# First 256 MLP features in plain products, in two token halves, and block sums on VectorE alone

## The chip, the cores and the metric

The kernel runs on one core of a Trainium2 chip. The metric is the device time of one execution in microseconds (us); before the change the median of three runs is 1396.17 us. TensorE (PE in the profile) multiplies, VectorE (DVE), ScalarE (ACT) and GpSimd (POOL) work on tiles, SyncE (SP) issues most transfers between HBM and the on-chip memory (SBUF). Each engine runs its own queue in order and waits on semaphores.

## What is computed

One layer of a hybrid encoder trunk on 1024 tokens with 1024 channels, in float32. The change lies between the output projection and the second MLP matrix:

```python
h = h + einsum('bse,ed->bsd', concat([y_a, y_b]), w_out)
z = einsum('bsd,df->bsf', rms_norm(h, norm2_g), w_ff1)      # 1024 -> 4096
h = h + einsum('bsf,fd->bsd', square(relu(z)), w_ff2)       # 4096 -> 1024
gate = sigmoid(einsum('bsd,de->bse', rms_norm(h, ple_norm_g), w_ple_gate))
h = h + gate * einsum('bsk,kd->bsd', p, w_ple_up)
```

## The kernel before, in words

Every float32 operand is split into a rounded high half (ScalarE, names ending in h) and the rest as a low half (VectorE, ending in l), and a product is three passes on TensorE: high x high, high x low, low x high. A matmul is 128x128 weights times 128x512 tokens.

The first MLP matrix (4096 features) is made in 16 blocks of 256 features, c = 0 to 15, from `products` and `sw_prods`. A block is a 2 x 2 split of features and channels against a 2 x 2 split of channels and tokens, done with seven products in place of eight (Strassen-Winograd): 7 products x 4 channel tiles x 3 passes = 84 matmuls. The token side (`sw_blocks`, four channel tiles j, each with its partner j + 4) has own blocks 11, 21, 22 and sums t1 to t4, all scaled by norm2_g, with a high and a low half; they stay in SBUF for all blocks. The weight side is made anew for each block (`sw_prep`): two raw transfers of 512 KB into tag wr (three buffers), own blocks a, sums s1 to s4 in four adds on SBUF (L231 to L234; on VectorE for c < 2, on GpSimd after that), and the split halves a, b, c, d in tags wh and wl (two buffers each).

The norm's factor is not needed before the end of a block: squares of h are summed in acc2 (L1198, L1199; ScalarE squares, GpSimd adds), `sumsq_to_rstd` sums over channels with small matmuls (tile n2ps) and takes the root, `bcast_rstd` spreads it with eight transposes (n2R) into Rb, and `finish(c)` multiplies relu(z) by it, squares, makes the sums that the second matrix wants (GpSimd, L1292 to L1298) and writes them to HBM (zd). The second matrix (`ff2_sweep`) reads them back (zr), its operands for three steps being fetched ahead by `ff2_early`.

In the last part of the output projection, products of channels 6 and 7 (op) run while the own blocks and sums of the first tiles are made. The order on each engine is set by a scheduler of the framework from program order and priorities; L1304 to L1346 are that program order.

Of the kernel before, what the change touches and what calls it, by code (L numbers as in the profile page):

```python
# [11 lines left out]
F32 = mybir.dt.float32  # L12
# [47 lines left out]
def tile_block(ctx, tc, xT, pT, w_in, w_out, w_ff1, w_ff2, w_gate, w_up, vecs, gate_b, rpbp, con,  # L60
# [179 lines left out]
        put(s1, 512, ("s1",), "d")  # L240
        return w

    def sw_prods(nm, w, B, z, part, ps_):


        pss = {}

        def prod(an, bn, js=range(4)):
            ps = pss.get(an)
            if ps is None:  # L250
                ps = pss[an] = ps_(f"{nm}_{an}_{bn}")
            elif js[-1] == 3:
                js = (3,)
            for j in js:
                for i, (x_, y_) in enumerate(passes(w[an][0][:, j], w[an][1][:, j], *B[bn, j])):
                    TE.matmul(ps, x_, y_, start=j == 0 and i == 0, stop=j == 3 and i == 2)  # L256
            return ps

        def add(o, a, b):
            mark["add"] = V.tensor_tensor(o, a, b, op=ALU.add).ins  # L260

        c11, c12, c21, u2 = z[0][:, 0:512], z[0][:, 512:], z[1][:, 0:512], z[1][:, 512:]
        if part == 2:
            for an, bn in (("11", "11"), ("12", "21"), ("s2", "t2"), ("s4", "22")):
                prod(an, bn, range(3))
        if part != 1:
            S.activation(u2, prod("11", "11"), AF.Copy)
            add(c11, u2, prod("12", "21"))
            add(u2, u2, prod("s2", "t2"))
        if part:  # L270
            add(c12, u2, prod("s4", "22"))
            add(u2, u2, prod("s3", "t3"))
            add(c21, u2, prod("22", "t4"))
            p5 = prod("s1", "t1")
            add(c12, c12, p5)
            add(u2, u2, p5)
# [912 lines left out]

    with tc.tile_pool(name="ff1", bufs=1) as ff1:  # L1190
        B = {}
        acc2 = utile32("acc2")

        sqs = []

        def sq_acc(acc, src):
            sqs.append(sqs[-2] if len(sqs) > 1 else utile32(f"sq2_{len(sqs)}"))
            S.activation(sqs[-1], src, AF.Square)  # L1198
            G.tensor_tensor(acc, acc, sqs[-1], op=ALU.add)  # L1199

        def b_alloc(nm, j):
            if len(B) < NB:
                t_ = ff1.tile([P, 2, 512], F32R, tag="b", bufs=NB, name=f"b{nm}_{j}")
            else:
                t_ = utile(f"b{nm}_{j}").rearrange("p (a b) -> p a b", a=2)
            return t_[:, 0], t_[:, 1]

        def blocks(j):
            h1, h2 = hres[j], hres[j + 4]
            tmp = utile32 if j > 1 else lambda n: wp.tile([P, T], F32, tag="wr", name=n, bufs=3)  # L1210
            sw_blocks(j, h1, h2, vcol(V_G2, j), vcol(V_G2, j + 4), tmp(f"ta{j}_"), tmp(f"tb{j}_"), b_alloc, B, True, G if j < 3 else V)
        def squares(ks):
            for k in ks:
                if k == 0:
                    S.activation(acc2, hres[k], AF.Square)
                else:
                    sq_acc(acc2, hres[k])
# [91 lines left out]
        blocks(0)  # L1309
        w4 = out_w((6, 7), range(4, 8))  # L1310
        run(out_proj((6, 7), range(4), ps_, w5))
        blocks(1)
        last = out_proj((6, 7), range(4, 8), ps_, w4)
        run(last, 25)
        squares((0, 4))
        blocks(2)
        run(last)
        w = prep(0)
        squares((1, 5))
        blocks(3)  # L1320
        squares((2, 6))
        with after("hi"):
            squares((3, 7))
        for e in range(8):
            dump(f"h1_{e}", hres[e])

        for c in range(NC_):
            if c:
                products(c, w, 0)
            else:  # L1330
                products(0, w, 2)
            if c == NC_ - 1:
                pre = [ff2_early(0)]
            if c == 1:
                bcast_rstd(rs2, range(KT), "n2")
                finish(0)
            if c:
                products(c, w, 1)
            else:
                rs2 = sumsq_to_rstd(acc2, range(KT), "n2")  # L1340
            if c + 1 < NC_:
                w = prep(c + 1)
            if c == NC_ - 1:
                pre += [ff2_early(1), ff2_early(2)]
            if c:
                finish(c)  # L1346


    with tc.tile_pool(name="ff2", bufs=2) as ff2:
# [226 lines left out]
```

## Time and profile before

| | us |
|---|---|
| median of 3 runs | 1396.17 (1395.35 to 1396.94) |
| the profiled execution | 1398.95 |
| its span in the trace | 1397.1 |
| mean granted clock of TensorE | 0.966 of full speed |
| TensorE busy | 1321.2 |
| VectorE busy | 914.1 |
| ScalarE busy | 591.5 |
| GpSimd busy | 545.7 |

TensorE's matmuls are pipelined: a row gives 0.39 us for one, but they start every 0.2267 us. A row of the timeline has a start, a duration, engine, line, operation, the tile written and the tiles read, and in brackets the idle time before it and the instruction whose end ended it.

### The profile page before, as it was taken

How to read it: one execution, taken by the hardware profiler on the slowest of the kernel's cores; microseconds unless marked ns; L12 is line 12 of the kernel's file. 1: busy time of each engine (PE TensorE's matmuls, PEld its weight loads, DVE VectorE, ACT ScalarE, POOL GpSimd, SP SyncE). 2: the span in 40 equal slices, each digit the busy share in tenths (PEclk: the TensorE clock that was granted, in tenths of full speed). 3: DMA queues.
4: the chain of work that ended last, by engine and by line, in shares of the span. 5: the costliest groups of instructions: out<-in, count | busy, mean ns of one | idle time of the engine just before them, and what ended most of it. 6: DMA issues, size and time to landing. Idle time of an engine off the chain costs nothing.

```text
span 1397.1 us, 19354 instructions
## 1 busy us (share of the span) xinstructions
PE 1321.2 (95%) x7115; PEld 1105.5 (79%) x7115; DVE 914.1 (65%) x1419; ACT 591.5 (42%) x971; POOL 545.7 (39%) x424
## 2 busy tenths in 40 slices
PE   7999999999998899996899999999999799999998
PEld 5988778799897667775678888888788678888887
DVE  4486886665672555669856666666648998559443
ACT  7353434264553545545333333333434334455321
POOL 2215676463331111116466555655202561007422
PEclk9999999999998799998899999999999999999999
DMA  8553333475322553311145444554876673542342
GB/s 288 198 152 83 117 112 106 149 250 165 112 62 99 168 165 129 117 48 45 32 165 160 141 150 136 159 166 158 303 273 224 196 254 94 171 147 72 106 143 83
DMA packets 153422, 206.03 MB, mean 147 GB/s; under 512 B 17776, under 2 KB 102768, under 8 KB 153328
## 3 DMA queue, kind: packets, MB, share of 16 engines
q1 hardware_dynamic: 144656, 185.77, 42.1%
q10 hardware_dynamic: 7200, 13.11, 2.8%
q0 software_dynamic: 1472, 5.92, 1.2%
q8 instruction: 56, 0.92, 0.3%
q14 instruction: 38, 0.31, 0.1%
HBM read 151.60 MB, written 53.17 MB: 147 GB/s over the span
## 4 chain that ended last, share of the span: by engine, by line
PE 56%; DMA 6%; DVE 6%; issue 3%; POOL 1%; ACT 1%; SPq 1%; DVEq 0%; POOLq 0%; ACTq 0%
PE f_P L1379 19%; PE p_s_t L256 9%; PE g L1448 6%; PE p L256 6%; PE op L1023 3%; PE p_s L256 3%; PE p_t L256 3%; DMA tab<-tabI 2%; PE pv L995 1%; DMA tab<-tabU 1%; PE o1p L310 1%; DMA nr<-qnd 1%; DMA wo_0r<-w_out 1%; DVE h L1025 1%; PE pt L975 1%
## 5 line engine op out<-in xcount | busy, mean ns | idle before, releaser
L1268 DVE TENSOR_TENSOR zl<-zr,zh 128x1024 fp32r<-128x1024 f32 x56 | 82.5, 1480 | 6.3 <-ACT zh L1267 6.3
L256 PE MATMUL p<-b,w_ah 128*128 128x512 f32 x256 | 80.3, 395 | 4.2 <-DVE b L193 4.2
L964 POOL TENSOR_SCALAR pc<-pc,st 128x288 f32<-128x288 f32 (+1 forms) x32 | 17.5, 548 | 160.9 <-DVE st L959 143.8
L1249 POOL TENSOR_TENSOR w2re<-sk,w2re 128x512 f32<-128x512 f32 x16 | 27.0, 1687 | 98.7 <-issue 62.9
L1267 ACT ACTIVATE zh<-zr 128x1024 fp32r<-128x1024 f32 x56 | 58.5, 1048 | 12.8 <-DMA zr<-zd 11.9
L260 DVE TENSOR_TENSOR z<-z,p_s_t 128x512 f32<-128x512 f32 x64 | 42.5, 686 | 32.2 <-PE p_s_t L256 30.9
L954 ACT ACTIVATE pc<-pc,st 128x288 f32<-128x288 f32 (+1 forms) x64 | 36.3, 569 | 57.6 <-DVE st L953 57.6
L256 PEld LDWEIGHTS p<-b,w_ah 128*128 128x128 f32 x256 | 48.7, 190 | 14.7 <-DVE b L193 4.6
L256 PE MATMUL p<-b,w_al 128*128 128x512 f32 x128 | 50.7, 398 | 9.3 <-DVE w_al L141 9.3
L1379 PE MATMUL f_P<-zl,w2h 128*128 128x512 f32 x128 | 52.3, 408 | 6.3 <-DVE zl L1268 6.3
L953 DVE CUSTOM_DVE_ANT_1 pc<-sc,tab 128x288 f32<-128x288 f32 (+1 forms) x64 | 29.9, 504 | 42.0 <-DMA tab<-tabU 17.6
L1402 POOL TENSOR_TENSOR h<-h,evP 128x512 f32<-128x512 f32 x8 | 14.8, 1886 | 98.3 <-ACT evP L1393 98.3
L788 POOL TENSOR_SCALAR wv<-vh,wj 128x129 f32<-128x129 f32 x56 | 30.6, 549 | 56.7 <-PE num L789 51.9
L1292 POOL TENSOR_TENSOR tz<-z,z 128x512 f32<-128x512 f32 x16 | 20.7, 1296 | 81.6 <-ACT z L1281 81.6
L1379 PE MATMUL f_P<-zh,w2h 128*128 128x512 f32 x128 | 51.1, 399 | 1.2 <-ACT zh L1267 1.2
L1448 PE MATMUL g<-gh,wg_h 128*128 128x512 f32 (+1 forms) x136 | 51.6, 380 | 0.0
L1379 PE MATMUL f_P<-zh,w2l 128*128 128x512 f32 x128 | 51.4, 401 | 0.0
L1448 PE MATMUL g<-gh,wg_l 128*128 128x512 f32 (+1 forms) x136 | 51.3, 377 | 0.0
L1448 PE MATMUL g<-gl,wg_h 128*128 128x512 f32 (+1 forms) x136 | 51.2, 377 | 0.0
L1280 DVE SCALAR_TENSOR_TENSOR z<-z,Rb 128x1024 f32<-128x1024 f32 x32 | 50.2, 1573 | 0.9 <-ACT Rb L180 0.9
L138 ACT ACTIVATE w_bh<-w_0r 128x1024 fp32r<-128x1024 f32 x16 | 17.0, 1063 | 73.0 <-POOL w_0r L234 53.3
L138 ACT ACTIVATE w_ah<-w_0r 128x1024 fp32r<-128x1024 f32 x16 | 17.0, 1061 | 68.4 <-PE p_t L256 68.4
(697 smaller groups left out, 4619.6 us busy)
## 6 DMA issues: line engine op xcount, KB each, us to landing
zr<-zd SPq DMA_DIRECT2D x56, 512.0 KB
zd<-z ACTq DMA_DIRECT2D x48, 256.0 KB
w2r<-w_ff SPq DMA_DIRECT2D x48, 256.0 KB
w_0r<-w_ff SPq DMA_DIRECT2D x16, 512.0 KB
w_1r<-w_ff SPq DMA_DIRECT2D x16, 512.0 KB
zd<-tz SPq DMA_DIRECT2D x32, 256.0 KB
zd<-z SPq DMA_DIRECT2D x32, 256.0 KB
w2re<-w_ff SPq DMA_DIRECT2D x16, 512.0 KB
```

What stands on the lines that cost most here:

```text
L138: mark["hi"] = S.activation(hi, raw, AF.Copy).ins
L256: TE.matmul(ps, x_, y_, start=j == 0 and i == 0, stop=j == 3 and i == 2)
L260: mark["add"] = V.tensor_tensor(o, a, b, op=ALU.add).ins
L788: G.tensor_scalar(wv, vh[:, c, 0:129], wj[:, col], 1.0, op0=ALU.mult, op1=ALU.mult)
L953: V.tensor_tensor_reduce(pb, sc.rearrange("p a b -> p (a b)"), tab[:, s], -1.0, -NEG, ALU.add, ALU.min, st[:, 0:1])
L954: S.activation(pb, pb, AF.Exp, scale=-1.0, bias=st[:, 0:1], accum_out=st[:, 1:2])
L1023: TE.matmul(ps, a, b, start=n == 0 and i == 0, stop=n == len(ks) - 1 and i == 2)
L1267: S.activation(hi, raw, AF.Copy)
L1268: dv.append(V.tensor_tensor(lo, raw, hi.bitcast(F32), op=ALU.subtract).ins)
L1280: V.scalar_tensor_tensor(z_, z_, 0.0, Rb, op0=ALU.max, op1=ALU.mult)
L1379: pe_last = TE.matmul(ps[n, e], a, b, start=st and k == 0, stop=sp and k == 2)
L1448: TE.matmul(ps, x_, y_, start=k == 0 and i == 0, stop=k == KT - 1 and i == 2)
```

## The change

Block 0 no longer uses sums. Its 256 features are computed as plain products, one token half (`plain("p0a")`, tokens 0 to 511, that is blocks 11 and 21 of the token side) right behind the output projection, before block 1, the other (`plain("p0b")`) behind block 15; 48 matmuls each. p0a's result is written to HBM and read back when the factor is known (in c = 3), and once more at the end to make block 0's sums. p0b (tokens 512 to 1023) needs block 22 and the blocks 12, made in c = 15 (four tiles), and its own copy of the weights, w1q.

`sw_blocks` is split into `own_blocks` (needed by p0a) and `sum_blocks`; all sums and low halves of the token side are on VectorE, and some are one 1024-wide instruction where two 512-wide ones stood. The squares come behind t1 of the last tile (`squares`), are added up in Rb itself, the first half of each on GpSimd and the second on VectorE, with one work tile. The norm's sum is taken in c = 2 behind its first three products, and it is spread, and block 1 finished, in the middle of the remaining products of c = 2.

```diff
-        def blocks(j):
-            h1, h2 = hres[j], hres[j + 4]
...
+        def own_blocks(j):
...
+            S.activation(hi, h2, AF.Copy, scale=g2)
+            V.scalar_tensor_tensor(lo, h2, g2, hi.bitcast(F32), op0=ALU.mult, op1=ALU.subtract)
+            B["21", j], B["22", j] = (h21, l21), (h22, l22)
+        def sum_blocks(j):
...
+            S.activation(t3, b12, AF.Copy, scale=g1)
+            V.scalar_tensor_tensor(t3, b22, g2, t3, op0=ALU.mult, op1=ALU.subtract)
+            V.scalar_tensor_tensor(t2, b11, g1, t3, op0=ALU.mult, op1=ALU.add)
+            V.scalar_tensor_tensor(t4, b21, g2, t2, op0=ALU.mult, op1=ALU.subtract)
+            (h2_, h4_, hi), (l2_, l4_, lo) = b_alloc(f"th_{j}"), b_alloc(f"tl_{j}")
+            S.activation(hi, tb, AF.Copy)
+            V.tensor_tensor(d1, b12, b11, op=ALU.subtract)
+            V.tensor_tensor(lo, tb, hi.bitcast(F32), op=ALU.subtract)
...
+        def squares():
+            sq = utile32("sq2")
+            for k in range(KT):
+                for half in range(2):
+                    hs = slice(half * 512, (half + 1) * 512)
+                    S.activation((sq if k else Rb)[:, hs], hres[k][:, hs], AF.Square)
+                    if k:
+                        (V if half else G).tensor_tensor(Rb[:, hs], Rb[:, hs], sq[:, hs], op=ALU.add)
...
+        w = plain_w("w1p")
+        run(last)
+        own_blocks(3)
+        z0 = utile32("z0a")
+        plain("p0a", w, bs("11"), bs("21"), ((0, 4), (1, 5), (2, 6), (3, 7)), (z0[:, h1_], z0[:, h0]))
+        nc.sync.dma_start(zd[2][:, 0], z0)
+        for j in range(2):
+            sum_blocks(j)
+        w = prep(1)
+        for j in range(2, 4):
+            sum_blocks(j)
+        with after("t1"):
+            squares()
...
+        for c in range(1, NC_):
+            products(c, w, 0)
+            if c == 2:
+                rs2 = sumsq_to_rstd(Rb, range(KT), "n2")
...
+            def spread():
                 bcast_rstd(rs2, range(KT), "n2")
-                finish(0)
...
+                finish(1)
+            sw_prods(f"p{c}", w, B, zt[c], 1, ps_, spread if c == 2 else None)
+            w = prep(c + 1) if c + 1 < NC_ else plain_w("w1q")
...
+        pre = [ff2_early(0)]
+        zb, z0 = utile32("z0c"), utile32("z0d")
+        plain("p0b", w, b12, bs("22"), ((4, 5, 6, 7), (0, 1, 2, 3)), (zb[:, h0], zb[:, h1_]))
+        nc.sync.dma_start(z0, zd[2][:, 0])
```

Three places show how instructions stand on their engines. The first is VectorE at the start of the first block with sums. Before, the rows behind the low half of the first weights (w_0_al) are:

```order
L193 SCALAR_TENSOR_TENSOR bt_2_6720<-ta__6699,vec,bt_2_6720 128x512
L1025 TENSOR_TENSOR h_6545<-h_6545,op_7_1_6739 128x512
L141 TENSOR_TENSOR w_0_al<-w_0_0r,w_0_ah 128x1024
L231 TENSOR_TENSOR s_0_6753<-w_0_1r 128x512
L193 SCALAR_TENSOR_TENSOR b_3_6785<-h_4998,vec,b_3_6785 128x512
L232 TENSOR_TENSOR w_0_1r<-w_0_0r,w_0_1r 128x512
```

Now, where w1p are the plain weights, ta and tb the work tiles of the sums, btl a low half of t2 and t4:

```order
L141 TENSOR_TENSOR w1p_1l<-w1p_1r,w1p_1h 128x1024
L1210 SCALAR_TENSOR_TENSOR b2l_6701<-h_6544,vec,b2h_6700 128x1024
L1225 TENSOR_TENSOR ta__6758<-h_4825 128x512
L141 TENSOR_TENSOR w_1_al<-w_1_0r,w_1_ah 128x1024
L1220 SCALAR_TENSOR_TENSOR ta__6758<-h_5137,vec,ta__6758 128x512
L233 TENSOR_TENSOR w_1_0r<-s_1_6792,w_1_0r 128x512
L1221 SCALAR_TENSOR_TENSOR tb__6759<-h_4825,vec,ta__6758 128x512
L1225 TENSOR_TENSOR ta__6775<-h_4888 128x512
```

Before, three of the four tiles' sums stand ahead of the first weights' low half; now one subtraction of tile 0 does, and all other sums stand behind it.

The second place is GpSimd between the end of the attention and block 3. Before, its rows mix block sums (L190, L207) and squares, and then go to block 2's weights (w_2):

```order
L190 TENSOR_TENSOR bt_2_6724<-tb__6700,bt_2_6724 128x512
L1199 TENSOR_TENSOR acc_6470<-acc_6470,sq_1_6778 128x1024
L207 TENSOR_TENSOR ta__6783<-h_4998 128x512
L1199 TENSOR_TENSOR acc_6470<-acc_6470,sq_0_6696 128x1024
L1199 TENSOR_TENSOR acc_6470<-acc_6470,sq_1_6778 128x1024
L1199 TENSOR_TENSOR acc_6470<-acc_6470,sq_0_6696 128x1024
```

Now, with sq the one work tile of the squares:

```order
L1245 TENSOR_TENSOR Rb<-Rb,sq_6851 128x512 x2
L231 TENSOR_TENSOR s_2_6983<-w_2_1r 128x512
L232 TENSOR_TENSOR w_2_1r<-w_2_0r,w_2_1r 128x512
L1245 TENSOR_TENSOR Rb<-Rb,sq_6851 128x512 x3
L233 TENSOR_TENSOR w_2_0r<-s_2_6983,w_2_0r 128x512
L234 TENSOR_TENSOR w_2_0r<-w_2_0r 128x512
L1245 TENSOR_TENSOR Rb<-Rb,sq_6851 128x512 x2
L171 TENSOR_TENSOR n2rs<-n2ms,mhalf 128x8
```

The block sums are gone from it, and the squares' adds now stand among block 2's weight sums.

The third place is SyncE's queue at the start of the second matrix (w2r its weights, zr its tokens, zd_108 the array in HBM that they come from). Before:

```order
L1235 DMA w2r_2_9107<-w_ff 128x512
L1266 DMA zr_0_9018<-zd_108 128x1024
L1287 DMA zd_109<-z_1_8833 128x512
L1235 DMA w2r_2_9107<-w_ff 128x512
L1266 DMA zr_1_9088<-zd_108 128x1024
L1266 DMA zr_3_9214<-zd_108 128x1024
```

Now:

```order
L1285 DMA w2r_2_9130<-w_ff 128x512 x2
L1316 DMA zr_3_9235<-zd_108 128x1024
L1316 DMA zr_0_9043<-zd_108 128x1024
L1338 DMA zd_106<-tz_9033 128x512
L1338 DMA zd_107<-tz_9033 128x512
```

The fetch of step 3's tokens moved ahead of those of step 0.

## Rows read from the trace of the kernel before

**Rows 1.** The page: busy time and share of the engines, and the chain by engine.
```profile
PE 1321.2 (95%) x7115; PEld 1105.5 (79%) x7115; DVE 914.1 (65%) x1419; ACT 591.5 (42%) x971; POOL 545.7 (39%) x424
PE 56%; DMA 6%; DVE 6%; issue 3%; POOL 1%; ACT 1%; SPq 1%; DVEq 0%; POOLq 0%; ACTq 0%
```

**Rows 2.** Stretches: length, busy time (instructions) by engine, granted clock, DMA share, GB/s.
```profile
660.00:665.00 5.00, 3.11 (x7) 2.51 (x8) 5.00 (x3) 1.06 (x1) 5.00 (x3) 0.50 0.00 0
...
675.00:680.00 5.00, 5.00 (x15) 3.96 (x16) 5.00 (x8) 3.11 (x6) 0.00 (x0) 0.64 0.35 101
...
740.00:960.00 220.00, 220.00 (x972) 182.25 (x971) 140.16 (x150) 73.46 (x82) 135.60 (x94) 1.00 0.49 157
```

**Rows 3.** TensorE's timeline, 627 to 713 us: start, duration, line, idle before.
```profile
627.66 0.39 PE L1023 MATMUL op<-yh,wo_6h 128*128 128x512 f32 x1
...
639.00 0.39 PE L1023 MATMUL op<-yh,wo_6h 128*128 128x512 f32 x1
641.21 0.50 PE L1023 MATMUL op<-yh,wo_6l 128*128 128x512 f32 x1 [1.83 <-DVE wo_6l L141]
...
661.89 0.80 PE L256 MATMUL p<-b,w_al 128*128 128x512 f32 x1 [9.27 <-DVE w_al L141]
...
671.88 0.80 PE L256 MATMUL p<-b,w_ah 128*128 128x512 f32 x1 [4.19 <-DVE b L193]
...
674.90 1.22 PE L256 MATMUL p_s_t<-bt,w_bh 128*128 128x512 f32 x2 [1.79 <-ACT w_bh L138]
...
690.39 1.84 PE L167 MATMUL n2ps<-ones,acc 128*128 128x1 f32 x16
...
712.35 0.62 PE L256 MATMUL p<-b,w_ah 128*128 128x512 f32 x2
```

**Rows 4.** VectorE's timeline, 659 to 680 us, with the neighbours by which pitches go.
```profile
659.07 2.77 DVE L141 TENSOR_TENSOR w_al<-w_0r,w_ah 128x1024 fp32r<-128x1024 f32 x1
...
663.43 2.86 DVE L193 SCALAR_TENSOR_TENSOR b<-h,vec,b 128x512 fp32r<-128x512 f32 x1
...
675.61 1.21 DVE L141 TENSOR_TENSOR w_bl<-w_0r,w_bh 128x1024 fp32r<-128x1024 f32 x1
676.74 1.22 DVE L141 TENSOR_TENSOR w_cl<-w_1r,w_ch 128x1024 fp32r<-128x1024 f32 x1
...
678.48 0.68 DVE L190 TENSOR_TENSOR bt<-ta__6783,bt 128x512 fp32r<-128x512 f32 x1
679.08 0.74 DVE L193 SCALAR_TENSOR_TENSOR bt<-ta__6783,vec,bt 128x512 fp32r<-128x512 f32 x1
679.75 0.68 DVE L190 TENSOR_TENSOR bt<-tb__6784,bt 128x512 fp32r<-128x512 f32 x1
```

**Rows 5.** GpSimd's timeline, 662 to 718 us.
```profile
662.92 8.36 POOL L1199 TENSOR_TENSOR acc<-acc,sq 128x1024 f32<-128x1024 f32 x3
...
707.04 1.30 POOL L1292 TENSOR_TENSOR tz<-z,z 128x512 f32<-128x512 f32 x1
...
710.80 2.28 POOL L1296 TENSOR_TENSOR z<-z 128x512 f32<-128x512 f32 x1
...
714.29 2.27 POOL L233 TENSOR_TENSOR w_0r<-s,w_0r 128x512 f32<-128x512 f32 x1
```

**Rows 6.** TensorE's timeline, block 2 and the start of the second matrix.
```profile
719.07 0.73 PE L256 MATMUL p_s_t<-bt,w_bh 128*128 128x512 f32 x2 [1.12 <-ACT w_bh L138]
720.33 0.50 PE L256 MATMUL p_s_t<-bt,w_bl 128*128 128x512 f32 x1 [0.53 <-DVE w_bl L141]
...
981.99 0.49 PE L1379 MATMUL f_P<-zh,w_0h 128*128 128x512 f32 x1 [0.70 <-ACT w_0h L138]
...
984.04 0.50 PE L1379 MATMUL f_P<-zh,w_0l 128*128 128x512 f32 x1 [1.23 <-DVE w_0l L141]
```

**Rows 7.** ScalarE's timeline, a rounding 1024 wide and one 512 wide.
```profile
673.79 1.06 ACT L138 ACTIVATE w_bh<-w_0r 128x1024 fp32r<-128x1024 f32 x1 [6.34 <-DVE w_0r L234]
...
676.22 0.61 ACT L189 ACTIVATE bt<-ta__6783 128x512 fp32r<-128x512 f32 x1
```

**Rows 8.** The chain of waits at the hand-over: start, us, what.
```profile
974.83 5.08 DMA zr<-zd
```

More of the change, by code (lines that the diff above doesn't have):

```diff
@@ L241, in sw_prep, with sw_prods @@
         return w
-    def sw_prods(nm, w, B, z, part, ps_):
+    def sw_prods(nm, w, B, z, part, ps_, mid=None):
         pss = {}
@@ L272, in sw_prods @@
             add(u2, u2, prod("s3", "t3"))
+            if mid:
+                mid()
             add(c21, u2, prod("22", "t4"))
@@ L1191, in tile_block @@
         B = {}
[L1192 to L1206, printed above, removed]
@@ L1208, in blocks @@
-        def blocks(j):
-            h1, h2 = hres[j], hres[j + 4]
[L1210 to L1217, printed above, removed]
+        nb = [0]
@@ new lines, in sum_blocks @@
+        def sum_blocks(j):
+            h1, h2, g1, g2 = hres[j], hres[j + 4], vcol(V_G2, j), vcol(V_G2, j + 4)
+            b11, b12, b21, b22 = h1[:, 0:512], h1[:, 512:], h2[:, 0:512], h2[:, 512:]
+            ta, tb = utile32(f"ta{j}_"), utile32(f"tb{j}_")
+            d1, t3, t2, t4 = ta[:, 0:512], ta[:, 512:], tb[:, 0:512], tb[:, 512:]
+            S.activation(t3, b12, AF.Copy, scale=g1)
[6 more added lines that the diff above has]
+            V.tensor_tensor(lo, tb, hi.bitcast(F32), op=ALU.subtract)
+            B["t2", j], B["t4", j] = (h2_, l2_), (h4_, l4_)
+            hi, lo, _ = b_alloc(f"t3_{j}")
+            S.activation(hi, t3, AF.Copy)
+            V.tensor_tensor(lo, t3, hi.bitcast(F32), op=ALU.subtract)
+            B["t3", j] = hi, lo
+            hi, lo, _ = b_alloc(f"t1_{j}")
+            S.activation(hi, d1, AF.Copy, scale=g1)
+            mark["t1"] = V.scalar_tensor_tensor(lo, d1, g1, hi.bitcast(F32), op0=ALU.mult, op1=ALU.subtract).ins
+            B["t1", j] = hi, lo
@@ new lines, in squares, with plain_w @@
+        def squares():
[6 more added lines that the diff above has]
+                        (V if half else G).tensor_tensor(Rb[:, hs], Rb[:, hs], sq[:, hs], op=ALU.add)
+        def plain_w(nm):
+            w = {}
+            for f in range(2):
+                r = wp.tile([P, T], F32, tag="wr", name=f"{nm}_{f}r", bufs=3)
+                nc.sync.dma_start(r.rearrange("p (k n) -> p k n", n=P), wview(w_ff1, 0, 8, f * P, (f + 1) * P))
+                w[f] = [t_.rearrange("p (k n) -> p k n", n=P) for t_ in split(wp, r, T, "w", f"{nm}_{f}")]
+            return w
@@ new lines, in plain @@
+        def plain(nm, w, B1_, B2_, order, z):
+            pss = [ps_(f"{nm}_{f}") for f in range(2)]
+            for n, ks in enumerate(order):
+                for f in range(2):
+                    for k in ks:
+                        b = B1_[k] if k < 4 else B2_[k - 4]
+                        for i, (x_, y_) in enumerate(passes(w[f][0][:, k], w[f][1][:, k], *b)):
+                            TE.matmul(pss[f], x_, y_, start=n == 0 and k == ks[0] and i == 0,
+                                      stop=n == len(order) - 1 and k == ks[-1] and i == 2)
+            for f in range(2):
+                S.activation(z[f], pss[f], AF.Copy)
@@ L1302, in out_w, with relu2 @@
             return w_split(w_raw(es, ks), es, ks)
+        def relu2(z, hs):
+            V.scalar_tensor_tensor(z, z, 0.0, Rb[:, hs], op0=ALU.max, op1=ALU.mult)
+            S.activation(z, z, AF.Square)
         w4 = out_w(range(6), (7,))
@@ L1308, in tile_block @@
         out_res(7)
-        blocks(0)
+        own_blocks(0)
         w4 = out_w((6, 7), range(4, 8))
         run(out_proj((6, 7), range(4), ps_, w5))
-        blocks(1)
+        own_blocks(1)
         last = out_proj((6, 7), range(4, 8), ps_, w4)
         run(last, 25)
-        squares((0, 4))
-        blocks(2)
+        own_blocks(2)
+        w = plain_w("w1p")
         run(last)
[L1318 to L1323, printed above, removed]
+        own_blocks(3)
```

56 lines of the change are left out of this document (36 added, 20 removed).

## The prediction

> **What bounds the kernel now.** I read the page first. TensorE is busy for 95% of the span and holds 56% of the chain that ended last, VectorE 6% [rows 1]. So time can only come from stretches in which TensorE waits, and the next thing to find is where those lie. The table by stretches puts them at the entry to the first MLP matrix: from 740 to 960 us TensorE is busy for all of the 220 us at full clock, while 660 to 665 shows 3.11 of 5 us at a granted clock of 0.50 and 675 to 680 a clock of 0.64 [rows 2]. TensorE's own timeline then gives the waits one by one [rows 3]. Its pitch is plain where nothing waits: 50 matmuls lie between the rows at 627.66 and 639.00, so 0.2267 us each. After that stand the waits: 1.83 us before 641.21 (weights of the output projection, VectorE), 9.27 before 661.89 (the low half of the first feature weights, VectorE), 4.19 before 671.88 (the last token block, VectorE), 1.79 before 674.90 (ScalarE's rounding of the weight sums). Block 0 ends at 690.39.
>
> How much of it is idle: from 627.66 to 690.39 are 62.73 us. In them lie 96 matmuls of the output projection and 84 of block 0, 180 x 0.2267 = 40.80. **21.9 us** are lost (waits, and what the lowered clock adds). VectorE sets that: no releaser on the long waits is another engine, and its instructions there last 2.77 us (1024 wide, 659.07) and 2.86 us (512 wide, 663.43) where the same forms last 1.21 and 0.74 a little later [rows 4]. GpSimd runs adds on SBUF tiles at those two moments and not at the later ones; when it runs against VectorE its own 512-wide add lasts 2.27 to 2.28 us in place of 1.30 [rows 5].
>
> After block 0, block 1 (690.39 to 712.35) holds 84 matmuls (19.04), 16 small ones for the norm (1.84) and eight transposes, which leaves some 0.4 us of waiting; block 2 waits 1.12 and 0.53 us for the weight sums [rows 3, 6]. Blocks 3 to 14 wait for nothing. The hand-over to the second matrix waits about 2.4 us: 0.70 and 1.23 as the rows count it, with the issue around them [rows 6].
>
> **Part 1: twelve more matmuls.** Block 0 is now 2 x 48 plain matmuls where the seven products were 84. 12 x 0.2267 = **+2.72 us**; none of it can hide, TensorE being the bound.
>
> **Part 2: the start.** VectorE and ScalarE run their rows in the order in which they stand, and that order is what I walk, with the pitches of rows 4: 0.66 us for a 512-wide scalar_tensor_tensor, 0.60 for a 512-wide tensor_tensor, 1.13 for a 1024-wide one, all without GpSimd beside them, because GpSimd now has no block sums at all. The second low half wo_6l is in time (GpSimd no longer slows it), so the projection ends at 627.66 + 96 x 0.2267 = 649.4. p0a needs only own blocks and w1p. VectorE reaches w1p_1l at about 652.6, since s_1 (ahead of it in its queue) waits for a weight transfer; TensorE loses 0.7 us, and p0a ends at 661.2.
>
> Then comes the place that costs the most. w_1_ah needs the buffer of w1p_0h, which p0a reads until about 660.0; ScalarE makes it in 1.06 us [rows 7]. VectorE has w_1_al, which needs w_1_ah, **ahead of all 31 rows of the block sums**. It stands idle from 653.7 to 661.15, 7.5 us, with work behind the wait that has its operands. From there: 16 x 0.66 + 9 x 0.60 + 6 x 1.13 = 22.7 us, and 3.6 us in which it waits for ScalarE's high halves between them, so the t1 of tile 3 is ready at 687.5. Behind it stand the first square's add and w_1_dl (2.3 us, to 689.8), and block 1's last product needs w_1_dl from its third matmul on: 11 more, and block 1 ends at 692.35. Idle from 627.66: 64.69 - 228 x 0.2267 (96 + 48 + 84) = 13.0 us, where it was 21.9. **-8.9 us.** Neither side of this is free: without the wait of 7.5 us it would be some -14, and if VectorE is slowed as in rows 4 at three of these rows, about -4. I take the walk, since nothing on GpSimd runs before 687.
>
> Granted clock: single waits in this walk stay under 3.6 us, and the row after the 4.19 us wait shows 0.64 [rows 2, 3]. At half clock some 2.5 us of matmuls would cost 1.2, but a wait for VectorE follows each time and takes it up. I count 0 and keep 1.2 for the range.
>
> **Part 3: the squares.** They now start behind t1, at 687.5, while blocks 1 and 2 run, and share three queues with block 2's weights. One work tile serves all tiles, so the first halves go one after another: a square on ScalarE (0.61, rows 7), an add on GpSimd (1.30, rows 5), with 0.2 between, 2.1 us a round. ScalarE has w_2_ah behind the third round's squares: 693.9, 1.55 us after TensorE wants it at 692.35. GpSimd has s_2 and w_2_1r behind round 2 and the last two weight sums behind round 5: 688.1 + 5 rounds and two more adds = 699.4, + 2 x 1.30 = 702.0, then w_2_bh in 1.06: 703.1. TensorE has done its 24 matmuls with w_2_a by 699.35 and waits 3.8 us. Block 2: 1.55 + 3.8 and small change = 5.4, where block 1 had 0.4: +5.0. In block 3 finish(1) comes late, because the norm's factor is spread only in the middle of block 2; its two GpSimd sums stand between the weight sums of block 3, and w_3_bh is 3.5 us late where block 2 lost 1.65 before: +1.9. Together **+6.9 us**.
>
> These adds were taken at 1.30. Of the rows of GpSimd between 707 and 718, two of eight last 2.27 to 2.28 [rows 5]. Nine of its adds lie on the way to w_2_bh; VectorE has one wide operation on SBUF in that time (w_2_al) and halves of 0.6. So I price one collision, 0.98 us: **+1.0**; the ends are 0 (none) and 4.4 (half of the nine, rounded up).
> The Trainium skill (SBUF — State Buffer, section "SBUF: two separate sides") says that a VectorE operation with two SBUF inputs and a GpSimd operation that reads SBUF exclude one another for the whole instruction. The rows at 659.07 and 663.43 agree with it (2.77 and 2.86 against 1.21 and 0.74), and it speaks against handing one half of each square's add to either engine: by it every round would collide, 0.68 us more on each of seven rounds, and the sum would be about 4 us higher.
>
> **Part 4: the hand-over.** The tiles of the second matrix take the memory of the token blocks. On SyncE the load zr_3 now stands ahead of zr_0 and waits until p0b's 24th matmul has read its block, 5.44 us after block 15's end. zr_0 goes out behind it; a load of that kind took 5.08 us [rows 8], so it lands near 11, after p0b's own 10.88 us; zh_3 and zh_0 follow at 1.06 each on ScalarE, and the first product starts 2.0 us late. In step 1 another 2.05 us goes, because ScalarE has w_2_2h, which waits for step 0's end, ahead of zh_1. 4.0 where 2.4 to 2.5 were lost: **+1.55**. If zr_0 lands within p0b it is -2.4, and if the loads share the queues badly +3.
>
> **Sum.** +2.72 - 8.9 + 6.9 + 1.0 + 1.55 = **+3.3 us**. The walk uses the profiled execution (span 1397.1, 1398.95 us with what lies around it), which is 2.8 us above the median of the runs; the difference is put on the median, 1396.17 + 3.3 = **1399.4 us**. A measurement of this kernel can tell about 0.2% (2.8 us) from no change, so this is just past that line.
>
> **Rivals.**
> A, the sum above: what the start gives is given back within two blocks. It gives 1399.4, with 2.5 either way. 0.55, of it slower 0.30, same 0.22, faster 0.03.
> B, faster: the waits move but do not add up. For it: blocks 3 to 14 show that this pipeline hides its weight sums once it has its lead [rows 2], and all of Part 3 hangs on three queues meeting within 5 us. If GpSimd has its two sums done before TensorE's 24 matmuls end, Part 3 shrinks to w_2_ah's 1.55 less the 2.05 lost before, with the hand-over as walked: 2.72 - 8.9 - 0.5 + 1.55 = -5.1, 1391. Against it: the sums stand behind five rounds that cannot go faster than 2.1 us. 0.20 (faster 0.17, same 0.03).
> C, slower than A by one mechanism: GpSimd and VectorE collide in most rounds of the squares. The price is 0.98 for each of the nine adds less the one counted; at half of them +7, at all +11. It decides from the fourth collision. For it: six adds of squares in before lasted up to 2.8 each (three in 8.36 us, rows 5). Against: those were 1024 wide, so 1.4 for a half. 0.17, at 1403.
> D, even: only the hand-over and block 3 come out as before, 2.72 - 8.9 + 5.0 + 1.0 = -0.2, 1396. 0.08.
>
> **The numbers.** Faster 0.17 + 0.03 = 0.20; same 0.22 + 0.03 + 0.08 = 0.33; slower 0.30 + 0.17 = 0.47. The range reaches to B on one side, 1391.0, and past C's first half on the other, 1404.5; about 1 in 10 stays out at each end.
>
> **What would show it.** In the profile after: VectorE idle for some 7 us before w_1_al; t1's last low half near 687.5 and block 1's end near 692.4 (Part 2); GpSimd adds L1245 in seven rounds of about 2.1 us, and TensorE waits of over 3 us for w_2_bh (Part 3); the first f_P some 2 us after p0b's last matmul, and a second wait in the step after (Part 4). If TensorE loses under 1 us in blocks 2 and 3, it is B; if the adds L1245 last over 2 us, it is C. The prediction is wrong at its root if VectorE does not stand before w_1_al.

## The result and the profile after

The changed kernel takes 1413.3 us (median of four runs, 1409.76 to 1415.03); the kernel before 1395.76 (the three runs named ahead and a fourth beside it, 1392.57 to 1396.94). The ratio is 1.0127, with a 95% interval of 1.0107 to 1.0146: 17.5 us slower. The forecast was 1399.4, with a range of 1391 to 1404.5. The side was right; the time lies 14 us above the forecast and 9 above the range.

The profiled execution took 1412.78 us, with a span of 1411.0. The page's first row and its chain by engine, which answer to [rows 1]:

```profile
PE 1327.6 (94%) x7127; PEld 1104.7 (78%) x7127; DVE 906.3 (64%) x1423; ACT 596.5 (42%) x980; POOL 523.4 (37%) x414
...
PE 36%; issue 6%; POOL 2%; DVE 2%; DMA 1%; ACT 1%; SPq 0%; POOLq 0%; DVEq 0%; ACTq 0%
```

TensorE has twelve matmuls more (7127 for 7115) and is busy 6.4 us longer, where twelve at the plain pitch are 2.7. The rest is not more work: a matmul at half clock counts as busy for longer (0.63 us at 703.43 below, 0.39 at 624.10), and how much half clock an execution has differs upstream of the change too. GpSimd is busy 22 us less, which the time doesn't show.

The table by stretches (as [rows 2]: length, then busy time and instructions of PE, PEld, DVE, ACT, POOL, granted clock, DMA share, GB/s) puts the loss in three places: 695 to 705, 720 to 735, and 990 to 1005. Between 760 and 960 TensorE is as full as before, but for 0.6 us.

```profile
695.00:700.00 5.00, 1.67 (x8) 1.06 (x6) 2.99 (x5) 1.77 (x3) 4.22 (x4) 0.98 0.00 0
700.00:705.00 5.00, 3.81 (x8) 2.61 (x9) 3.77 (x4) 4.27 (x6) 2.76 (x3) 0.50 0.21 59
...
720.00:730.00 10.00, 6.43 (x29) 4.91 (x27) 6.31 (x6) 1.60 (x3) 9.51 (x6) 1.00 0.34 131
730.00:735.00 5.00, 4.48 (x14) 3.38 (x13) 2.86 (x3) 3.03 (x4) 2.89 (x2) 0.66 0.83 251
...
760.00:960.00 200.00, 199.41 (x878) 164.45 (x877) 130.92 (x141) 66.07 (x73) 121.24 (x84) 1.00 0.48 152
990.00:995.00 5.00, 4.42 (x10) 3.51 (x11) 4.45 (x5) 3.25 (x6) 1.28 (x1) 0.50 0.68 216
```

TensorE's timeline (start, duration, line, tiles, idle before), to be laid beside [rows 3] and [rows 6]. The rows without a bracket at 657.06, 689.49, 720.37 and 745.51 are the first matmuls of blocks 1 to 4, and the one at 975.21 is p0b's:

```profile
624.10 0.39 PE L1025 MATMUL op<-yh,wo_6h 128*128 128x512 f32 x1
...
657.06 0.62 PE L256 MATMUL p<-b,w_ah 128*128 128x512 f32 x2
...
674.84 0.50 PE L256 MATMUL p_s_t<-bth,w_bh 128*128 128x512 f32 x1 [2.74 <-ACT bth L1224]
...
681.21 0.50 PE L256 MATMUL p_s_t<-bth,w_bh 128*128 128x512 f32 x1 [2.18 <-ACT bth L1224]
...
687.08 0.50 PE L256 MATMUL p_s_t<-bt,w_dl 128*128 128x512 f32 x1 [0.70 <-DVE w_dl L141]
...
689.49 0.63 PE L256 MATMUL p<-b,w_ah 128*128 128x512 f32 x2
...
691.84 0.50 PE L256 MATMUL p<-b,w_al 128*128 128x512 f32 x1 [1.26 <-DVE w_al L141]
...
701.15 0.79 PE L256 MATMUL p_s_t<-bth,w_bh 128*128 128x512 f32 x1 [4.48 <-ACT w_bh L138]
...
703.43 0.63 PE L256 MATMUL p_s_t<-btl,w_bh 128*128 128x512 f32 x1
703.86 0.63 PE L256 MATMUL p_s_t<-bth,w_bl 128*128 128x512 f32 x1
...
720.37 0.62 PE L256 MATMUL p<-b,w_ah 128*128 128x512 f32 x2
...
729.54 0.50 PE L256 MATMUL p_s_t<-bth,w_bh 128*128 128x512 f32 x1 [3.57 <-ACT w_bh L138]
...
745.51 0.61 PE L256 MATMUL p<-b,w_ah 128*128 128x512 f32 x2
...
975.21 0.39 PE L1264 MATMUL p0b<-b2h,w1q_0h 128*128 128x512 f32 x1
...
990.58 2.93 PE L1457 MATMUL f_P<-zh,w_0h 128*128 128x512 f32 x6 [2.81 <-ACT zh L1317]
...
1001.06 1.88 PE L1457 MATMUL f_P<-zh,w_1h 128*128 128x512 f32 x7 [1.87 <-ACT zh L1317]
```

A stage's length goes from its first matmul to the next stage's. Block 2, say, is 720.37 - 689.49 = 30.88 us, where 84 plain matmuls are 19.04. Block 2's wait of 4.48 us is followed by matmuls 0.43 us apart (703.43 to 703.86), which is the pitch of half clock, where 0.2267 is plain. Half clock is counted below as what matmuls without a wait ahead of them take above 0.2267 each, and waits as the same for those with one. The whole difference, from the first matmul with wo_6h to the end, laid against the sum of the prediction (the start as the prediction counts it, in time above plain matmuls; block 2 against before's stretch from block 0's end to block 1's, 21.96 us, and block 3 against its block 2, since these hold the norm and finish):

| us against before | forecast | measured |
|---|---|---|
| twelve matmuls more | +2.72 | +2.72 |
| start, to block 1's end | -8.9 | -8.2 |
| block 2 (with collisions) | +6.0 | +8.9 |
| block 3 | +1.9 | +3.9 |
| block 5 | 0 | +1.2 |
| hand-over, p0b to the end of the second matrix | +1.55 | +8.6 |
| behind that | 0 | +0.3 |
| sum | +3.3 | +17.4 |

Upstream of it the profiled execution ran 3.6 us ahead of the one of before (624.10 against 627.66 in [rows 3]), so the two profiled times differ by 13.8 only; the medians differ by 17.5, near the table's 17.4.

### The profile page after: what moved, and what is told of

The parts are those of the page before. It is cut to its first block, busy times and chain, and to the rows that moved or that the text cites. A ratio compares the mean times of both kernels' runs of the same rounds, so it can differ in the third digit from the quotient of the medians.

```text
span 1411.0 us, 19381 instructions
## 1 busy us (share of the span) xinstructions
PE 1327.6 (94%) x7127; PEld 1104.7 (78%) x7127; DVE 906.3 (64%) x1423; ACT 596.5 (42%) x980; POOL 523.4 (37%) x414
## 5 line engine op out<-in xcount | busy, mean ns | idle before, releaser
L966 POOL TENSOR_SCALAR pc<-pc,st 128x288 f32<-128x288 f32 (+1 forms) x32 | 17.5, 545 | 159.2 <-DVE st L961 137.1
L1299 POOL TENSOR_TENSOR w2re<-sk,w2re 128x512 f32<-128x512 f32 x16 | 32.0, 1999 | 104.9 <-DVE sk L1298 94.5
L1331 ACT ACTIVATE z<-z 128x1024 f32<-128x1024 f32 x30 | 31.8, 1060 | 22.8 <-DVE z L1330 22.2
L256 PE MATMUL p_s_t<-bth,w_bh 128*128 128x512 f32 x60 | 25.4, 424 | 14.5 <-ACT w_bh L138 9.6
L141 DVE TENSOR_TENSOR w_cl<-w_1r,w_ch 128x1024 fp32r<-128x1024 f32 x15 | 21.7, 1444 | 27.0 <-ACT w_ch L138 27.0
```

Source lines behind the costliest of these rows:

```text
L1299: G.tensor_tensor(a21, s1, a11, op=ALU.subtract)
```

## The experiments

All ratios are to the kernel before, beside which each was run; the changed kernel's own is 1.0127 (1.0107 to 1.0146). The two kernels on the squares and the three with both halves at the start lie clear below that interval. The intervals of the others overlap with it, so what they tell comes from the stages of one trace each.

**The squares.** The smallest cut first: the squares of tiles 1 to 7 are left out.

```diff
-            for k in range(KT):
+            for k in range(1):
```

> The change without the squares of channel tiles 1 to 7 (only tile 0 is squared, so the norm's factor is wrong; 14 squares and 14 adds are left out). Theory (the squares' chain makes w_2_ah and w_2_bh late in block 2, and with it the lowered clock): block 2 falls from 30.9 us to about 22, block 3 keeps most of its waits because finish(1) is still in the middle of block 2; 7 to 10 us faster than the change, near 1405. Rival (block 2 waits for its own weight transfers and sums, whatever the squares do): under 2 us faster, 1412.

Measured: 1404.61 us, ratio 1.0062 (1.0041 to 1.0082), so 9 us less. Block 2 takes 21.78 in place of 30.88; block 3 stays at 25.20 and p0b with the second matrix at 340.2 (340.4). The squares make the whole of block 2's loss, and none of block 3's, where the wait stands as it was:

```profile
722.39 0.50 PE L256 MATMUL p_s_t<-bth,w_bh 128*128 128x512 f32 x1 [3.52 <-ACT w_bh L138]
```

Next the same sum with all its work, but otherwise placed: two work tiles, the adds 1024 wide and on VectorE alone, behind block 2's first weights, and the norm's sum behind that block's weight sums.

```diff
-                    S.activation((sq if k else Rb)[:, hs], hres[k][:, hs], AF.Square)
-                        (V if half else G).tensor_tensor(Rb[:, hs], Rb[:, hs], sq[:, hs], op=ALU.add)
+                S.activation(sq[k % 2] if k else Rb, hres[k], AF.Square)
+                    V.tensor_tensor(Rb, Rb, sq[k % 2], op=ALU.add)
...
+            if c == 1:
+                with after('t1', 'l2a'): squares()
```

> The change with nothing left out, but the squares' adds on VectorE alone (1024 wide, two work tiles) and behind w_2_al; GpSimd does only block 2's weight sums, and the root behind them. Theory (block 2 waits because its weight sums stand behind the squares' adds on GpSimd and its high halves behind the squares on ScalarE): w_2_bh is in time, block 2 takes 22 to 24 us where the change took 30.9, with no half clock in it; 6 to 9 us faster than the change, near 1406. Rival (what matters is that the squares are summed this late at all: the root then comes late and block 2 or 3 waits for it): block 2 shorter but block 3 longer by as much, within 3 us of the change.

Measured: 1404.66 us, 1.0057 (1.0041 to 1.0072). Block 2 takes 24.25, with no wait for w_2_bh any more; block 3 grows a little, from 25.14 to 26.03. So the squares' work as such did not have to cost 9 us: placed otherwise it costs 2.5 in block 2 and 0.9 in block 3. Several things were changed together (engine, place, width, number of work tiles), so how much is due to the adds' place among GpSimd's weight sums alone isn't shown.

**The clock.** Spare matmuls, whose results nothing reads, fill the waits before w_2_bh and w_3_bh and behind p0b: 16, 14 and 10 of them, and in a second kernel 25, 16 and 10.

```diff
+            for _ in range({('p2', 's2'): 16, ('p3', 's2'): 14}.get((nm, an), 0)): TE.matmul(ps, B['11', 0][0][:, 0:128], B['11', 0][0], start=True, stop=True)
...
+        for _ in range(10): TE.matmul(dum, b12[3][0][:, 0:128], b12[3][0], start=True, stop=True)
```

> The change, with spare matmuls that TensorE runs where it waited: 16 before the product of s2 in block 2 (a wait of 4.48 us there), 14 before the same product of block 3 (3.57 us), 10 behind p0b (2.81 us). They write a PSUM tile that the next product starts anew, so the result is the same and no wait ends later. Theory (the waits lower the granted clock, and the half clock behind them costs some 8 us: about 3.3 in block 2, 1.7 in block 3, 3.4 at the hand-over): clock 1.00 behind these waits and some 6 to 8 us faster than the change, near 1406. Rival (the clock falls for another reason, or TensorE's lost time is made up because it waits again): no difference, 1413.

Measured: 1408.43 us, 1.0106 (1.0069 to 1.0142). In block 3 a wait of 0.46 us is left, the clock stays at 1.00, and the block takes 23.80 in place of 25.14. In block 2 the sixteen don't reach: waits of 1.81 and 0.53 are left, and 0.73 is granted behind them. Rows of the table by stretches and of TensorE's timeline:

```profile
700.00:705.00 5.00, 3.37 (x8) 2.45 (x9) 3.82 (x4) 4.26 (x6) 2.70 (x2) 0.73 0.23 67
...
725.00:730.00 5.00, 4.43 (x19) 3.02 (x17) 1.48 (x2) 1.95 (x2) 4.26 (x3) 1.00 0.27 105
```

```profile
701.10 0.50 PE L257 MATMUL p_s_t<-bth,w_bh 128*128 128x512 f32 x1 [1.81 <-ACT w_bh L138]
...
702.36 0.79 PE L257 MATMUL p_s_t<-bth,w_bl 128*128 128x512 f32 x1 [0.53 <-DVE w_bl L141]
...
729.16 0.50 PE L257 MATMUL p_s_t<-bth,w_bh 128*128 128x512 f32 x1 [0.46 <-ACT w_bh L138]
```

> As the kernel with spare matmuls before (16, 14 and 10), with 25 ahead of the product of s2 in block 2 and 16 in block 3, so that no wait of over 1 us is left there. In block 2 the remaining wait of 1.81 us was still followed by half clock. Theory (the wait lowers the clock): clock 1.00 in block 2 behind w_2_bh, block 2 about 1.5 us shorter than with 16, though w_2_bh comes no earlier; near 1406, 1 to 2 us under the kernel with 16. Rival: half clock comes with w_2_bh whatever TensorE did before; no difference.

Measured: 1411.05 us, 1.0106 (1.0084 to 1.0128). With 25, the wait for w_2_bh is gone and the clock full:

```profile
700.00:705.00 5.00, 4.47 (x20) 3.29 (x19) 3.40 (x4) 4.21 (x6) 3.11 (x3) 1.00 0.14 39
```

Block 2 takes 29.32, 1.56 less than in the changed kernel, though its matmuls at half clock there lost 2.89: what the faster matmuls gain is in part waited for at the next tile (0.53 us for w_2_bl, at 702.76). Block 3 gives back 1.36 of 1.66, the hand-over 0.9 of 3.06, and block 5 took 0.5 more: 3.3 us in all (the ratios say 2.9, with intervals that overlap). At the hand-over the half clock was not removed. Behind the ten spare matmuls, waits of 0.93 and 1.38 us are left, 0.66 is granted, and 2.0 us of half clock stay:

```profile
990.00:995.00 5.00, 4.62 (x14) 3.69 (x14) 3.80 (x5) 1.60 (x3) 1.55 (x1) 0.66 0.82 252
```

So of the 7.6 us that half clock adds behind these three waits, some 5.4 were taken away, and 3.3 of them came out of the time.

**The start.** The plain weights w1p get tiles of their own, so that w_1_ah need not wait for p0a, and VectorE not for w_1_ah.

```diff
-        w = plain_w("w1p")
+        w = plain_w("w1p", True)
```

> The change with the split weights of p0a in tiles of their own, so that block 1's w_ah does not wait for p0a's end. Theory (VectorE's idle 6.6 us ahead of w_1_al moves all block sums, and these set block 1's end): VectorE runs through, block 1 ends some 6 us earlier, and the squares with it; 5 to 7 us faster than the change, near 1407. Rival (what is gained in block 1 is waited for again in blocks 2 and 3, where the squares and finish(1) decide): within 1.5 us of the change.

Measured: 1410.29 us, 1.0114 (1.0093 to 1.0135). Block 1 takes 29.52 in place of 32.43 and p0a 0.3 less; blocks 2 and 3 and the hand-over give 1.3 of that back. But VectorE did not run through. It stands idle as long as before, for another instruction: the first sum of tile 0 needs ScalarE's copy of ta, and in ScalarE's queue that stands behind the copy of p0a's result (z0a), which waits for p0a's end.

```profile
654.38 0.75 DVE L1220 SCALAR_TENSOR_TENSOR ta__6758<-h,vec,ta__6758 128x512 f32<-128x512 f32 x1 [6.82 <-ACT ta__6758 L1219]
```

```profile
653.14 0.60 ACT L1267 ACTIVATE z0a<-p0a 128x512 f32<-128x512 f32 x1 [7.59 <-PE p0a L1264]
```

So the 3.2 us are not the worth of the wait. They come with w_1_al, two weight sums and w_1_bl (some 3.5 us by the pitches of the prediction), which now stand ahead of the wait in place of behind it; the block sums start as late as they did. What the wait itself costs stays open: no kernel here has ScalarE's copy of ta ahead of z0a.

**The hand-over.** Two kernels. In the first, p0b comes ahead of block 15, so that the second matrix follows a block as it did before.

```diff
+            if c == NC_ - 1:
+                p0b(w)
+                w = prep(c)
...
+            if c == NC_ - 1:
+                pre += [ff2_early(1), ff2_early(2)]
```

> The change with p0b ahead of block 15 in place of behind it (blocks 12 made in block 14). Theory (the loads of the second matrix wait for p0b's reads and for what p0b keeps): the hand-over is as before the change, first f_P within 1.5 us of block 15's last product and no half clock behind it; 8.6 us of the hand-over become about 2, less what block 15's weights cost, whose buffers p0b's weights now hold: 4 to 6 us faster than the change, near 1408. Rival (the loads are late on SyncE for other reasons): no difference at the hand-over, and 1413 to 1416.

Measured: 1415.81 us, 1.0148 (1.0132 to 1.0164). p0b still takes 13.94 and block 15 now 25.82, its last stretch being a wait of 3.68 us for w_0h; the first tokens are fetched at 985.6, late again, now behind block 0's stores on SyncE: the time is the rival's. In the second kernel the fetch for step 3, and its halves, stand behind those of step 2, and p0b runs feature by feature.

```diff
+            with tc.issue_after(dv[-LAG]), (tc.issue_after(zdma[-1]) if (i, c) == (2, 3) else ExitStack()), (tc.issue_after(zact[-1]) if (i, c) == (2, 3) else ExitStack()):
```

> The change with another order at the hand-over alone: the load, the high half and the low half of step 3's tokens go behind those of step 2, and p0b runs one feature tile after the other, so that its first weight buffer is free after 24 matmuls in place of 36. Theory (the load of step 0 goes out late and shares the queues with step 3's, its weights wait for p0b's buffer, and ScalarE has the wrong half first): the first f_P starts within 1.5 us of p0b's last matmul, no half clock behind it, the 10.6 us lost at the hand-over and in its first steps fall to about 4; 5 to 7 us faster than the change, near 1407. Rival (the transfers themselves are slow, with two blocks' results and p0b's read-back under way): the load still lands some 6.7 us after its issue, and the gain is under 2 us.

Measured: 1410.13 us, 1.0106 (1.0073 to 1.0138). p0b takes 12.07 where it took 15.37: with step 3's fetch out of the way, zr_0 goes out 4.7 us after block 15 and lands nearly in time. Its load still takes 6.1 us (978.35 to 984.49), though no other fetch of tokens is beside it. And the second matrix takes 327.09 in place of 325.06, its wait having moved one step on:

```profile
997.62 2.93 PE L1458 MATMUL f_P<-zh,w_1h 128*128 128x512 f32 x6 [6.10 <-ACT zh L1318]
```

**Both halves at the start.** If the hand-over costs 8.6 us and the start gains, the plain half p0b may as well stand at the start, behind p0a; the squares then go as in the kernel with late squares.

```diff
+            plain2("p0", w, ((bs("11"), bs("21"), (z0[:, h1_], z0[:, h0])), (b12, bs("22"), (zb[:, h0], zb[:, h1_]))))
+            nc.sync.dma_start(zd[1][:, 0], zb)
...
-            plain("p0b", w, b12, bs("22"), ((4, 5, 6, 7), (0, 1, 2, 3)), (zb[:, h0], zb[:, h1_]))
```

> Both token halves of the first 256 features as plain products at the start (96 matmuls behind the projection, one feature tile after the other, the blocks 12 made there), their weights in tiles of their own, the squares as in the kernel that has them behind w_2_al; nothing is left for the end, so that the hand-over is as in the kernel before the change. Theory (the start is bound by VectorE's row of block sums, some 26 us, and 21.8 us of plain products cover it, where 10.9 did not; waits elsewhere come from queues, not from the idea): block 1 ends about 63 us after the first wo_6h with one more half block done, no wait of over 1 us in block 1, hand-over as before; 1380 to 1386, 10 to 15 us faster than before the change. Rival (the block sums are late whatever stands ahead, since VectorE now has the blocks 12 and both weight splits too): block 1 waits 5 us or more, and the time is 1390 or above.

Measured: 1400.37 us, 1.0025 (1.0011 to 1.0039). TensorE waits for almost nothing at the start, 41.52 us for both plain halves and block 1 (180 x 0.2267 = 40.8):

```profile
645.00:685.00 40.00, 39.74 (x175) 32.38 (x174) 28.72 (x39) 19.58 (x28) 1.82 (x2) 1.00 0.16 54
```

And then blocks 2 to 6 take 28.60, 24.86, 23.31, 22.39 and 20.22, and the hand-over 4.5 us more than before, with no p0b in it. VectorE still loses 7.0 us at the start, as with w1p in tiles of its own: ScalarE's copy of ta stands behind the copies of the plain products.

```profile
657.49 0.75 DVE L1221 SCALAR_TENSOR_TENSOR ta__6824<-h,vec,ta__6824 128x512 f32<-128x512 f32 x1 [7.01 <-ACT ta__6824 L1220]
```

Two more kernels only moved what stood in the way, and both keep that idle time (6.99 and 7.00 us). First the norm's sum, finish(1) and the read-backs of block 0:

```diff
+                with after('sum'): rs2.append(sumsq_to_rstd(Rb, range(KT), "n2"))
...
+            if c == 2:
+                with after('sum'): finish(1)
```

> The kernel with both token halves plain at the start, the weights of block 0 in tiles of their own and the squares on VectorE late (e7_start) took 41.5 us for blocks 0 and 1 with no wait worth naming, but 28.6, 24.9, 23.3, 22.4 and 20.2 for blocks 2 to 6, where 19.04 is plain: some 22 us of waits and of matmuls at half clock behind them. This kernel changes only where things stand: the norm's sum behind one more product of block 2 and its spreading behind two more, the finishing of block 1 behind the weights of block 3 on GpSimd and ScalarE, and the read-back of block 0's results a block later behind the weights. Theory (those waits are set by what stands ahead of the weight rows in the queues): block 2 23 to 25, block 3 20 to 21, blocks 4 to 6 near 19.1, so 12 to 15 us less than e7_start: 1386 to 1389, faster than before. Rival (the engines are simply full: VectorE and ScalarE have more work in these 100 us than fits, and what is moved out of one block waits in the next): the sum of blocks 2 to 6 stays over 112 us, and the time within 3 us of e7_start, 1397 to 1401.

Measured: 1399.04 us, 1.0007 (0.9988 to 1.0027). Blocks 2 to 7 take 27.08, 21.92, 21.56, 21.12, 22.72 and 23.74: 138.1 us, against 138.4. The rival's time held; that the engines are full, its reason, isn't shown by it. The second kernel uses the read-backs two blocks after they are issued:

```diff
+            if c == 5:
+                with after('add'):
+                    for hs in (h0, h1_):
+                        relu2(z0[:, hs], h0)
...
+            if c == 7:
+                with after('sum'):
+                    z_blocks(0, zb[:, h0], zb[:, h1_], z0[:, h1_], z0[:, h0])
```

> e9_order only moved the waits: blocks 2 to 7 together take 138.1 us there and 138.4 in e7_start, where 6 x 19.04 is 114.2. Its trace names one cause for blocks 4 to 7: VectorE and ScalarE stand before the read-back of block 0's results (5.3 us of waiting in one block, then 1.3 and 1.6 in the next), and behind them in their queues stand the weight halves of the next block; in block 6 GpSimd makes block 0's four sums ahead of the weight sums of block 8. Edit against e9_order: the read-backs are used two blocks after they are issued and behind the last product's adds, and block 0's sums stand behind the weight sums of block 8. Nothing else. Theory (a wait in a queue, not a full engine): blocks 4 to 7 take 77 to 80 us in place of 89.1, and the time falls by 9 to 12, to 1387 to 1390, 0.5 to 0.7% under before. Rival (without a lead of a block the weights are late anyway, because the chain from one block's products to the next block's weights is longer than 19 us): blocks 4 to 7 stay over 86, the time over 1396.

Measured: 1399.21 us, 1.0024 (1.0007 to 1.0041). Blocks 4 to 7 take 86.2, 3 us less than they did, and blocks 8 and 9, plain in the kernel above, 4.3 us more: the rival's time again. The trace names a resource. ScalarE's copy of a block's first product waits for a store to HBM to free a tile, and the next block's w_ah stands right behind it:

```profile
792.32 0.60 ACT L268 ACTIVATE z<-p 128x512 f32<-128x512 f32 x1 [5.40 <-DMA zd<-tz]
792.81 1.05 ACT L138 ACTIVATE w_ah<-w_0r 128x1024 fp32r<-128x1024 f32 x1
```

```profile
797.91 0.50 PE L257 MATMUL p<-b,w_al 128*128 128x512 f32 x1 [3.25 <-DVE w_al L141]
```

Results, stores and read-backs share one pool of 16 tiles in the kernel, so a tile that holds a read-back for longer is one that the blocks lack. None of these kernels beats the one before the change; these last two tie with the kernel before, within 0.25%.

## Why the prediction was right or wrong

The sum is some 14 us too low: 7.1 of them lie at the hand-over, 2.9 in block 2, 2.0 in block 3, 1.2 in block 5 and 1.0 elsewhere. Two steps failed. The larger is Part 4's walk of the fetch of zr_0 ("5.44 us after block 15's end", "a load of that kind took 5.08 us"), which put the hand-over at +1.55 where it measured +8.6. The other is the half clock behind long waits, put at 0.

**Part 1, right.** p0a and p0b have 96 matmuls, and the pitch is 0.2267.

**Part 2, right, by its mechanism and its size.** VectorE does stand before w_1_al, with the sums behind it, for 6.62 us (7.5 in the walk), and the last low half of the t1 of tile 3 ends at 684.72. The walk had 687.5 on a clock that starts 3.56 us later, that is 683.9. VectorE's timeline:

```profile
649.51 0.69 DVE L1225 TENSOR_TENSOR ta__6758<-h 128x512 f32<-128x512 f32 x1
656.81 1.23 DVE L141 TENSOR_TENSOR w_al<-w_0r,w_ah 128x1024 fp32r<-128x1024 f32 x1 [6.62 <-ACT w_ah L138]
...
682.93 1.79 DVE L1234 SCALAR_TENSOR_TENSOR bt<-ta__6834,vec,bt 128x512 fp32r<-128x512 f32 x1
```

Block 1 ends at 689.49, where the walk had 692.35 - 3.56 = 688.8. The half clock inside block 1 cost 3.5 us and was taken up by the waits for tiles, as the text said: the last of them, 0.70 us before 687.08, is for w_1_dl from VectorE. The bound "without the wait it would be some -14" stays untested, since the kernel meant to take the wait away kept it (6.82 us).

The walk left one thing out: "nothing on GpSimd runs before 687", which is 683.4 on this clock, did not quite hold. GpSimd's first add of squares starts at 682.89, and beside it the row at 682.93 lasts 1.79 us. In the kernel with late squares, where GpSimd is idle then, the same row lasts 0.75, and block 1 takes 31.57, 0.86 less.

**Part 3, the long wait right, the clock behind it priced at nothing.** The squares' adds run in rounds of about 2.04 us (693.66 to 695.70), the two weight sums stand behind five of them, and TensorE waits for w_2_bh:

```profile
682.89 1.28 POOL L1245 TENSOR_TENSOR Rb<-Rb,sq 128x512 f32<-128x512 f32 x1 [73.99 <-ACT sq L1243]
...
690.67 2.25 POOL L1245 TENSOR_TENSOR Rb<-Rb,sq 128x512 f32<-128x512 f32 x1
693.66 1.29 POOL L1245 TENSOR_TENSOR Rb<-Rb,sq 128x512 f32<-128x512 f32 x1 [0.74 <-ACT sq L1243]
695.70 1.29 POOL L1245 TENSOR_TENSOR Rb<-Rb,sq 128x512 f32<-128x512 f32 x1 [0.74 <-ACT sq L1243]
...
698.29 1.72 POOL L234 TENSOR_TENSOR w_0r<-w_0r 128x512 f32<-128x512 f32 x1
```

Waits take 6.06 us of block 2, where the walk had 5.4 and one collision at 0.98; in block 3 they take 4.43, where it had 3.5. That block 2 came so near is in part luck. The walk's wait of 1.55 us for w_2_ah on ScalarE did not come; the 1.26 us before 691.84 are for w_2_al on VectorE. And GpSimd began its first add 1.7 us before the walk (682.89, where 688.1 - 3.56 is 684.54) and ended the last weight sum 1.6 us behind it (700.01 for 698.44): its nine adds lasted 14.2 us, where 9 x 1.30 are 11.7, so they lost 2.5 us and not the 0.98 of one collision. Rival C wanted four collisions or more, 3.9 us, and fell with that; one of the nine lasts over 2 us (690.67). What was missing in both blocks is the other column: 2.89 and 1.66 us of half clock behind those two waits. The failed step here is the sentence "I count 0 and keep 1.2 for the range". It was right for the start, where another wait follows each time, and was carried over to Part 3, whose own waits of 3.8 and 3.5 us were just as long and had only short waits behind them. The row after the 4.19 us wait in [rows 2, 3] had shown it. The trace (0.50 granted behind the wait of 4.48 us, 0.66 behind that of 3.57) agrees with the Trainium skill (TensorE: Matmul & The Clock Gate, section "HAM oscillation — how this bites in real kernels"), which tells of a kernel whose TensorE waits for a transfer between groups of matmuls and starts each next group at the low clock. The spare matmuls show that the clock's net price in these two blocks is 2.9 us, not the 4.6 that the rows add up to.

Block 3's loss comes from finish(1) on GpSimd, as the walk had it. Two of its sums (L1346, L1349) stand ahead of the last weight sum, at 2.27 and 2.24 us each:

```profile
722.71 2.27 POOL L1346 TENSOR_TENSOR tz<-tz,z 128x512 f32<-128x512 f32 x1
724.94 2.24 POOL L1349 TENSOR_TENSOR z<-z 128x512 f32<-128x512 f32 x1
727.14 1.26 POOL L234 TENSOR_TENSOR w_0r<-w_0r 128x512 f32<-128x512 f32 x1
```

The loss stays without the squares, and block 3 falls from 24.86 to 21.92 in the first of the two kernels that go on from both halves at the start, where finish(1) stands behind these weight sums, with other things moved beside it.

**Block 5, not priced.** Block 5 takes 1.2 us more, with waits of 0.30 and 0.29 us for w_al and w_bl from VectorE, which had waited 0.97 us for the read-back of p0a's half and worked 2.4 us on it (755.90). That the read-back is the cause is argued from these rows; no run takes it out of there alone. The change names this transfer, and the working didn't walk it.

**Part 4, the term that was sized worst.** The chain of waits after the change (start, us, what), beside [rows 8]:

```profile
977.00 5.34 PE p0b L1264 x22
...
982.35 0.33 SPq L1316
...
982.73 6.71 DMA zr<-zd
...
989.47 1.06 ACT zh L1317
...
990.58 8.41 PE f_P L1457 x23
```

The order was the one forecast: zr_3 first, behind p0b's matmuls, and zr_0 behind it. But p0b's own weights came 1.2 us late (VectorE), so the two fetches went out 7.1 us after block 15, not 5.44; and the load of zr_0 took 6.71 us, not 5.08. Its company explains 0.6 of these 1.6 at most: in the kernel with the other order zr_0 goes alone and takes 6.1. The first product starts 15.4 us behind block 15's end, where 12.9 were forecast. Then 2.80 us of waits in step 1 (forecast 2.05), and 3.06 us of half clock behind the wait of 2.81 before the first product. The text's own bound, "if the loads share the queues badly +3", was the nearer value, and it was still too low, as neither the late weights nor the clock was in it. The kernel with the other order shows that the loss isn't in one wait: with step 0's fetch first, step 1 waits (6.10 us). How much of this is memory that block 15 and p0b still hold, and how much SyncE's order, stays open: in the three kernels without p0b at the end the hand-over still takes 4.3 to 5.6 us more than before.

**The rivals.** B, the faster one, fell by the rounds of the squares, as the text's "against it" said; D needed the hand-over as before. The range missed because its upper end was made of one mechanism (collisions), while three terms that were put at or near zero (clock, block 5, hand-over) all pointed upwards.

## What to carry to other kernels

TensorE's waits at the start of a pipeline may come back further down when they are filled. From the last projection step to the block where all is plain again, the time above plain matmuls (norm included) is 27.1 us in the kernel before, 32.9 in the changed one, 26.4 with late squares, and 24.9, 24.5 and 25.8 in the three kernels with both halves at the start; filling the first wait with useful matmuls moved most of it into the next blocks. That the other engines need this time in any case isn't shown, as VectorE stands idle for 6.6 to 7.0 us at the start of the changed kernel, of the one with late squares and of these three; the order without that idle time is the one to try next. So walk a gain at the start until the queues are again a block ahead, count what each long wait adds behind it in clock, and take the upper end of a range from all terms that were put at zero, together.

## What had not been expected of the hardware

A wait of 0.46 us left the clock at 1.00; waits of 2.81, 3.57 and 4.48 us were followed by stretches at 0.50 to 0.66 (and 0.73 behind 1.81 and 0.53). The length of the wait does not decide it by itself: behind 0.93 and 1.38 us in the kernel with more spare matmuls 0.66 was granted, while the changed kernel's waits of 1.87 and 0.93 (1001.06, 1003.87) lie in a stretch at 1.00 (1000 to 1005). And taking away some 5.4 of the 7.6 us of half clock won 3.3, because the matmuls at full speed ran in part into the next wait.
